# The decoder trunk's first loads merged with x transposed, and mem's norm factors summed on GpSimd

## The chip, the cores and the metric

One core of a Trainium2 chip runs the whole program; the metric is the device time of one execution in microseconds. Before the change three runs took 628.57, 625.1 and 627.83 us, median 627.83.

## The reference, cut to what matters

A decoder trunk of two layers on 256 tokens of width 1024. Each layer normalizes, mixes, adds, normalizes, and runs a gated feed-forward block:

```
xn = rms_norm(h, norm_mix[i]);  mn = rms_norm(mem, norm_mem[i])
mk, mv = split(mn @ w_mem_kv[i])                  # 4 memory heads, 256 memory tokens
proj = xn @ w_in                                  # q, k, v of 12 heads, memory queries, (layer 0) forget gates
self_out = fox_attention(...) or moba_attention(...)
h = h + concat(self_out, memory_attention(qm, mk, mv)) @ w_out[i]
gu = rms_norm(h, norm_ffn[i]) @ w_gate_up[i]
h = h + (silu(gate) * up) @ w_down[i]
```

where `rms_norm(x, g) = x * rsqrt(mean(x*x) + 1e-6) * g`. Layer 0 is the forgetting layer: its logits get a bias from the running sums of log-sigmoid gates. Everything is float32.

## The kernel before, in words

All weights come as one stream of units of about 1 MB, in the order of use; a unit fills one of four `raw` buffers. The tensor engine multiplies in a split form: each weight half-unit is copied by ScalarE to a rounded `hi` (L215) and VectorE forms `lo` = raw - hi (L216), and each product is three matmuls, hi by hi, lo by hi and hi by lo (`prod`, all at L178). Activations are split in the same way by `split_ps` (L237 on ScalarE, L238 on VectorE), scaled by the norm's gain. There are seven `hi` and seven `lo` buffers; `weights` splits five half-units ahead (AHEAD) and fetches three units ahead (FETCH). The norm's per-token factor is not applied to the operand: it is computed apart (`factor`: a ScalarE square with a sum at L243, VectorE L254, a GpSimd power at L256), turned into a row of factors for all partitions by `spread` (matmuls into `rsb_ps`, ScalarE L267), and multiplied into the products.

TensorE and SyncE (SP) run in the order in which the program is written. The order on ScalarE (ACT), VectorE (DVE) and GpSimd (POOL) is set ahead of time by a planner that puts what is ready first, and an engine never changes that order on the chip. SP issues the loads one after another, and a load whose buffer isn't free holds back all behind it.

Layer 0 runs on TensorE like this:
- eight warm matmuls on a zeroed tile (L737 clears it, after four clears of `mk` at L314);
- the value projection `v_ps`, 16 steps (eight row blocks k of x transposed, two token blocks t) of six matmuls. The stream's first unit is x transposed, loaded in four cuts; the value weights, units 1 to 4, are cut too, and cuts of the two are issued in turn. x's rows for the norm factors (`h`), the constants `sq` and the gate bias `bfg` come after unit 5;
- `qk_ps`, the first four heads' queries and keys (half-units of units 5 and 6), then `rsb_ps_x`;
- `mem_kv(0)`: memory keys and values `mk_ps`, `mv_ps`, from mem transposed (`x_mem`, unit 7, split at L237 and L238) and units 8 and 9. The gates' running sums (`F_ps`, `Fq_ps`) fall in the middle of it, at the second call of `step()`, which moves every generator in `active` on by one `yield`; the sums go to DRAM (`fd`, L490) and come back on all partitions (`fk`, three loads at L493);
- `qm_ps`, the memory queries; after its eight steps the last part of `mem_kv(0)`: mem's rows are loaded as a unit of their own (`U["mem"]`), squared on ScalarE (`junk_mem`, L243), and mem's factors give `rsb_ps_mem`; then `mk` is scaled (L349) and split in eight half-partition copies on ScalarE (L369, L370) and two differences (L372), the values are evacuated (L353), the memory queries are scaled (L535) and split (L362, and L364 on GpSimd and VectorE);
- the next `qk_ps` with the scores of the memory heads (`s_m`) and of the first self heads (`s_s`) between its steps, and so on; the bias of a head pair is four VectorE instructions at L510.

After some 133 us the feed-forward block of layer 0 begins, then layer 1; neither is touched by the change but for the buffers' size and what comes earlier or later from layer 0.

Of the kernel before, what the change touches and what calls it, by code (L numbers as in the profile page):

```python
# [45 lines left out]
HEAD = 384  # L46
WORK_BUFS = 7
PAIR_BUFS = 3
WARM = 8
FACTORS_AT = 6  # L50
# [28 lines left out]
class Plan:  # L79


    def __init__(self, a):
# [4 lines left out]
        U["xT"] = self.unit([xT], 0, KD, 0, S)  # L87
        for i in range(2):
# [3 lines left out]
            for u in range(4):  # L92
                U["vf", i].append(self.unit([w], 2 * u, 2, 2 * SW, nv))
            for g in range(3):
                if g == MEM_AT[i]:
                    if i == 0:
                        U["memT", 0] = self.unit([memT], 0, KD, 0, S)
                        self.mkv(a, 0)
                        self.blocks.append(a["mem"][0].reshape(NT, P, D).transpose(1, 0, 2).reshape(-1))
                        self.shapes.append((NT, 1, D))  # L100
                        U["mem"] = len(self.shapes) - 1
                    U["qm", i] = self.unit([w], 0, KD, 2 * SW + nv, MW)
# [36 lines left out]
def trunk(ctx: ExitStack, tc: tile.TileContext, plan, stream, x, gains, norm_final, b_fgate, square, out):  # L139
# [43 lines left out]
    raw_only = {U["xT"], U["memT", 0], U["memT", 1], U["mem"]}  # L183
# [3 lines left out]
    AHEAD, FETCH = 5, 3  # L187

    def fetch():
# [3 lines left out]
        raw = wp.tile([P, UNIT], F32, tag="raw", name=f"raw{i}", bufs=4)  # L193
# [12 lines left out]
    def split():  # L206
        i, k0, nk = halves[counts[1]]
        fetch_to(i + 1 + FETCH)
        sh = plan.shapes[i][1:]
        n = nk * sh[0] * sh[1]  # L210
        hi = wp.tile([P, HALF], F32R, tag="hi", name=f"hi{i}_{k0}", bufs=7)
        lo = wp.tile([P, HALF], F32R, tag="lo", name=f"lo{i}_{k0}", bufs=7)
        src = raws[i][:, k0:k0 + nk].rearrange("p a b c -> p (a b c)")
        for c0, c1 in ((0, HEAD), (HEAD, n)) if (i, k0) == (1, 0) else ((0, n),):
            nc.scalar.activation(hi[:, c0:c1], src[:, c0:c1], AF.Copy)  # L215
            nc.vector.tensor_sub(lo[:, c0:c1], src[:, c0:c1], hi[:, c0:c1].bitcast(F32))  # L216
# [75 lines left out]


# [22 lines left out]
    for mk in mks:  # L316
        no_lo(mk)
# [41 lines left out]
    def split_queries(dst, q):  # L359
# [3 lines left out]
        for a in range(2):  # L363
            ENG[a].tensor_sub(dst[HOME[1 - a], a], q[HOME[a]], dst[HOME[a], a].bitcast(F32))  # L364
# [68 lines left out]
    active = []  # L433

# [6 lines left out]
    def mixer(i, xs, rs):  # L441
# [11 lines left out]
        order = [(k, t) for k in range(KD) for t in range(NT)]  # L453
        if i == 1:
            order.sort(key=lambda kt: (kt[0] // 4, kt[1], kt[0]))
        for k, t in order:
            v_tile(k, t)
            if i == 0 and (k, t) == (FACTORS_AT, 1):
                rs.extend(factor(h[t_], f"x0{t_}") for t_ in range(NT))
        if i == 0:  # L460
            z = sp.tile([P, NT, H], F32, tag="z", name="z", bufs=1)
            for t in range(NT):
                nc.vector.scalar_tensor_tensor(z[:, t], vb[t][1].t[:, w0:w0 + H], rs[t], bfg, op0=ALU.mult, op1=ALU.add)
            na = sp.tile([P, NT, H], F32, tag="na", name="na", bufs=1)
            nc.vector.scalar_tensor_tensor(na, z, -1.0, z, op0=ALU.mult, op1=ALU.min)
            e = sp.tile([P, NT, H], F32, tag="e", name="e", bufs=1)
            nc.scalar.activation(e, na, AF.Exp)
            l = sp.tile([P, NT, H], F32, tag="l", name="l", bufs=1)
            nc.scalar.activation(l, e, AF.Ln, bias=1.0)
            lf = cp.tile([P, NT, H], F32, name="lf")  # L470
            nc.vector.scalar_tensor_tensor(lf, z, 0.0, l, op0=ALU.min, op1=ALU.subtract)
        for t in range(NT):
            for c in range(2):
                dst = vsb[t][:, 6 * c:6 * c + 6, 0:DH]
                src = vb[t][c].t[:, :w0].rearrange("p (a d) -> p a d", d=DH)
                if c == 0:
                    nc.scalar.activation(dst, src, AF.Copy, scale=rs[t])
                else:
                    nc.vector.tensor_scalar_mul(dst, src, rs[t])
# [3 lines left out]
        def gate_sums():  # L483
# [7 lines left out]
            for g in range(GATE_PARTS):  # L491
                hs = slice(g * (H // GATE_PARTS), (g + 1) * (H // GATE_PARTS))
                nc.sync.dma_start(fk[:, hs], fd[hs].unsqueeze(0).to_broadcast([P, H // GATE_PARTS, S]))  # L493
# [4 lines left out]
            nc.scalar.activation(fq.rearrange("p t h -> p (t h)"), gb.t[:, :NT * H], AF.Copy)  # L498

        def bias(h0):  # L500
# [7 lines left out]
            for a in range(2):  # L508
                for t, o in ((0, b0), (1, b)):
                    nc.vector.scalar_tensor_tensor(o[:, a], b[:, a, :(t + 1) * P], fq[:, t, h0 + a:h0 + a + 1], mask[:, P - t * P:],  # L510
                                                   op0=ALU.subtract, op1=ALU.add)
# [5 lines left out]
        def memory_heads():  # L517
# [269 lines left out]
```

## Time and profile before

| | us |
|---|---|
| median of three runs | 627.83 (625.1 to 628.57) |
| the profiled execution | 628.3 |
| its span, first to last instruction | 626.5 |
| busy in the span: PE, DVE, ACT, POOL | 609.5, 457.3, 392.6, 60.4 |
| mean granted TensorE clock | 0.992 |

The span is what the trace covers; 1.8 us of the profiled execution lie around it. A busy time is the time in which an engine has an instruction running, waiting for a port of the memory included.

### The profile page before, as it was taken

How to read it: one execution, taken by the hardware profiler on the slowest of the kernel's cores; microseconds unless marked ns; L12 is line 12 of the kernel's file. 1: busy time of each engine (PE TensorE's matmuls, PEld its weight loads, DVE VectorE, ACT ScalarE, POOL GpSimd, SP SyncE). 2: the span in 40 equal slices, each digit the busy share in tenths (PEclk: the TensorE clock that was granted, in tenths of full speed). 3: DMA queues.
4: the chain of work that ended last, by engine and by line, in shares of the span. 5: the costliest groups of instructions: out<-in, count | busy, mean ns of one | idle time of the engine just before them, and what ended most of it. 6: DMA issues, size and time to landing. Idle time of an engine off the chain costs nothing.

```text
span 626.5 us, 9569 instructions
## 1 busy us (share of the span) xinstructions
PE 609.5 (97%) x3636; PEld 536.2 (86%) x3636; DVE 457.3 (73%) x827; ACT 392.6 (63%) x734; POOL 60.4 (10%) x90
## 2 busy tenths in 40 slices
PE   7999899999999999999999999999999999999995
PEld 5999887778888888888899999877888888888884
DVE  5588899978676666668675589986876666676664
ACT  6679887666555555557466589875755555555542
POOL 2021345300000000000011033100000000000000
PEclk8999899999999999999999999999999999999999
DMA  8974812445555555555555633332455545555301
GB/s 293 390 283 166 347 69 85 146 173 202 199 174 179 194 196 202 194 177 176 210 186 194 215 140 126 135 134 68 169 201 202 186 176 181 198 201 202 136 0 67
DMA packets 17638, 112.31 MB, mean 179 GB/s; under 512 B 2220, under 2 KB 2744, under 8 KB 5432
## 3 DMA queue, kind: packets, MB, share of 16 engines
q1 hardware_dynamic: 17304, 111.42, 49.1%
q8 instruction: 28, 0.46, 0.3%
q10 hardware_dynamic: 288, 0.29, 0.1%
q14 instruction: 18, 0.15, 0.1%
HBM read 110.64 MB, written 1.06 MB: 178 GB/s over the span
## 4 chain that ended last, share of the span: by engine, by line
PE 83%; DVE 7%; ACT 6%; issue 2%; DMA 2%; POOL 0%; SPq 0%; POOLq 0%; ACTq 0%; DVEq 0%
PE gu L178 39%; PE d_acc L178 18%; PE qk_ps L178 8%; PE v_ps L178 6%; PE o_acc L178 4%; DVE lo L216 2%; DMA raw<-in_stream 2%; ACT hi L215 2%; PE s_s L178 1%; ACT p_s L406 1%; PE mv_ps L178 1%; PE qm_ps L178 1%; PE mk_ps L178 1%; PE s_m L178 1%; ACT xq L362 1%
## 5 line engine op out<-in xcount | busy, mean ns | idle before, releaser
L216 DVE TENSOR_TENSOR lo<-raw,hi 128x1024 fp32r<-128x1024 f32 (+3 forms) x201 | 240.6, 1204 | 70.6 <-ACT hi L215 65.6
L215 ACT ACTIVATE hi<-raw 128x1024 fp32r<-128x1024 f32 (+3 forms) x201 | 206.2, 1034 | 74.2 <-PE d_acc L178 47.0
L178 PE MATMUL gu<-x_ffn,hi 128*128 128x512 f32 x704 | 177.5, 392 | 0.0
L178 PEld LDWEIGHTS gu<-x_ffn,hi 128*128 128x128 f32 x704 | 126.3, 189 | 22.2
L178 PE MATMUL d_acc<-hi,h 128*128 128x512 f32 x348 | 107.1, 389 | 0.0
L178 PEld LDWEIGHTS gu<-x_ffn,lo 128*128 128x128 f32 x704 | 96.7, 190 | 8.1 <-ACT x_ffn L237 1.0
L178 PE MATMUL gu<-x_ffn,lo 128*128 128x256 f32 x704 | 100.5, 284 | 0.2
L178 PEld LDWEIGHTS d_acc<-hi,h 128*128 128x128 f32 x348 | 65.3, 188 | 13.6
L178 PE MATMUL qk_ps<-x_x,hi 128*128 128x256 f32 x384 | 73.7, 288 | 0.0
L178 PE MATMUL d_acc<-lo,h 128*128 128x512 f32 x174 | 67.7, 389 | 0.0
L178 PEld LDWEIGHTS qk_ps<-x_x,hi 128*128 128x128 f32 x384 | 62.1, 195 | 0.8 <-issue 0.8
L178 PE MATMUL qk_ps<-x_x,lo 128*128 128x256 f32 x192 | 55.0, 286 | 0.0
L642 ACT ACTIVATE gate<-gu 128x256 f32<-128x256 f32 x44 | 16.9, 384 | 57.6 <-PE gu L178 57.6
L178 PE MATMUL o_acc<-hi,x_hT 128*128 128x512 f32 x128 | 41.7, 404 | 0.6 <-DVE x_hT L235 0.3
L642 ACT ACTIVATE up<-gu 128x256 f32<-128x256 f32 x44 | 16.9, 385 | 40.0 <-PE gu L178 39.7
L178 PEld LDWEIGHTS d_acc<-lo,h 128*128 128x128 f32 x174 | 32.7, 188 | 6.8
L178 PEld LDWEIGHTS qk_ps<-x_x,lo 128*128 128x128 f32 x192 | 37.6, 196 | 0.0
L643 DVE TENSOR_TENSOR gate<-gu,gate 128x256 f32<-128x256 f32 x44 | 18.7, 424 | 25.8 <-ACT gate L642 25.8
L643 DVE TENSOR_TENSOR up<-gu,up 128x256 f32<-128x256 f32 x44 | 18.7, 425 | 25.1 <-ACT up L642 25.1
L178 PE MATMUL v_ps<-hi,x_x 128*128 128x384 f32 (+1 forms) x128 | 34.3, 350 | 1.7 <-ACT hi L215 1.7
L406 ACT ACTIVATE p_s<-p_s,nmax_s 128x128 f32<-128x128 f32 (+1 forms) x48 | 21.4, 446 | 11.8 <-DVE nmax_s L396 11.6
L178 PEld LDWEIGHTS o_acc<-hi,x_hT 128*128 128x128 f32 x128 | 22.8, 188 | 6.4 <-issue 1.3
(152 smaller groups left out, 752.3 us busy)
## 6 DMA issues: line engine op xcount, KB each, us to landing
raw<-in_stream SPq DMA_DIRECT2D x95, 1024.0 KB, 4.8
raw<-in_stream SPq DMA_DIRECT2D x4, 768.0 KB, 4.5
raw<-in_stream SPq DMA_DIRECT2D x2, 780.0 KB, 8.3
fk<-fd SPq DMA_DIRECT2D x3, 512.0 KB, 4.9
raw<-in_stream SPq DMA_DIRECT2D x3, 390.0 KB, 6.2
h<-in_x SPq DMA_DIRECT2D x2, 512.0 KB, 7.1
raw<-in_stream SPq DMA_DIRECT2D x1, 512.0 KB, 7.1
gfin<-in_norm_final SPq DMA_DIRECT2D x1, 512.0 KB, 3.7
```

The source lines that it names most:

```text
L178: nc.tensor.matmul(o, lhsT, rhs, start=self.fresh, stop=stop, skip_group_check=True)
L215: nc.scalar.activation(hi[:, c0:c1], src[:, c0:c1], AF.Copy)
L216: nc.vector.tensor_sub(lo[:, c0:c1], src[:, c0:c1], hi[:, c0:c1].bitcast(F32))
L362: nc.scalar.activation(dst[HOME[a], a], q[HOME[a]], AF.Copy)
L406: nc.scalar.activation(pr[:, a, c], src, AF.Exp, bias=nmax[:, a, j], scale=scale, accum_out=total[:, a, j])
L642: nc.scalar.activation(v[:, 1], b[s].t[:, S:], AF.Copy)
L643: nc.vector.tensor_add(v[:, 0], b[s].t[:, :S], v[:, 1])
```

## The change

- x transposed is no unit of its own any more: each of the four value units carries, for each row of weights, the 256 columns of x transposed ahead of the 780 of the weights (2,072 columns a unit, and `raw` grows from 2,048 to that). Unit 0 is loaded in two halves, the others whole. `split_first` splits x's row block between a half-unit's `hi` and its `lo`. SP issues the four units first, then `h`, `sq` and `bfg`.
- ACT and DVE follow the written order in layer 0's value stage: splitting runs at most two half-units ahead into the next stage, the values are evacuated before the gate's exponential and logarithm, and the factors of x are asked for at k = 2 and not 6. Warm matmuls: 12 for 8; GpSimd clears their tile before `mk`.
- The unit `mem` goes. Mem's squares come from mem transposed: on GpSimd eight products and seven sums of 128x256 (`mem_squares`), then two small matmuls by a column of minus ones add over the partitions (`mem_factors`). That is asked for after k = 1 of `qm_ps`, and the rest of `mem_kv(0)` after k = 4, where both came after k = 7.
- The three `fk` loads are issued two `step()` calls later, and the L510 instructions are queued behind the last split of the memory queries.

```
-WARM = 8
-FACTORS_AT = 6
+RAW = 2 * (S + SW + H)
+WARM = 12
+FACTORS_AT = 2
...
-        U["xT"] = self.unit([xT], 0, KD, 0, S)
...
+                cols = w[:, 2 * SW:2 * SW + nv]
+                if i == 0:
+                    cols = np.concatenate([xT, cols], axis=1)
+                U["vf", i].append(self.unit([cols], 2 * u, 2, 0, cols.shape[1]))
...
-                        U["mem"] = len(self.shapes) - 1
...
-        cuts = {0: [0, n // 8, n // 4, n // 2, n], 1: [0, HEAD, n // 2, n], 2: [0, n // 2, n]}.get(i, [0, n])
+        cuts = [0, n // 2, n] if i == 0 else [0, n]
...
             nc.scalar.activation(hi[:, c0:c1], src[:, c0:c1], AF.Copy)
+            if with_x and c0 == 0:
+                split_first(i, k0)
             nc.vector.tensor_sub(lo[:, c0:c1], src[:, c0:c1], hi[:, c0:c1].bitcast(F32))
...
-        while counts[1] < min(len(halves), ready[i, kk][2] + 1 + AHEAD):
+        while counts[1] < min(len(halves), ready[i, kk][2] + 1 + ahead[0]):
...
+    x0 = xposed("x0")
+    def split_first(i, kk):
+        k = 2 * U["vf", 0].index(i) + kk
+        split_ps(x0[0][:, k, :], x0[1][:, k, :], raws[i][:, kk, 0, :S], gT[:, k, 0:1])
...
+    def mem_squares():
+        w = cp.tile([P, 2, S], F32, name="squares")
+        for k in range(KD):
+            src = raws[U["memT", 0]][:, k, 0, :]
+            nc.gpsimd.tensor_mul(w[:, min(k, 1)], src, src)
+            if k > 0:
+                nc.gpsimd.tensor_add(w[:, 0], w[:, 0], w[:, 1])
+        return w[:, 0]
+    def mem_factors(sums):
+        b = bank("ms_mem")
+        for t in range(NT):
+            b.mm(b.t[:, 2 * t:2 * t + 2], sums[:, t * P:(t + 1) * P], prefix[:, P:P + 2], stop=True)
+        for t in range(NT):
+            me = sp.tile([P, 1], F32, tag="me", name=f"me_mem{t}")
+            nc.vector.tensor_scalar(me, b.t[:, 2 * t:2 * t + 1], -1.0 / D, EPS, op0=ALU.mult, op1=ALU.add)
+            rs = sp.tile([P, 1], F32, tag="rs", name=f"rs_mem{t}", bufs=8)
+            nc.gpsimd.tensor_tensor(rs, me, minus_half, op=ALU.pow)
+            rs_mem.append(rs)
...
         split_x(U["memT", i], 2 + i, xs, range(MEM_AHEAD))
+        if i == 0:
+            sums = mem_squares()
         yield
...
-            fetch_to(U["mem"] + 1)
-            rs_mem.extend(factor(raws[U["mem"]][:, t, 0], f"mem{t}") for t in range(NT))
+            mem_factors(sums)
+            yield
...
+        with tc.manual_schedule(engines={ACT, DVE}) if i == 0 else nullcontext():
...
+                if i == 0:
+                    ahead[0] = min(AHEAD, KD + 1 - k)
...
-            for g in range(GATE_PARTS):
-                hs = slice(g * (H // GATE_PARTS), (g + 1) * (H // GATE_PARTS))
-                nc.sync.dma_start(fk[:, hs], ...)
             gb = bank("Fq_ps")
...
+            yield
+            yield
+            for g in range(GATE_PARTS):
+                hs = slice(g * (H // GATE_PARTS), (g + 1) * (H // GATE_PARTS))
+                nc.sync.dma_start(fk[:, hs], ...)
...
+                    with tc.issue_after(mem_done[i]):
+                        nc.vector.scalar_tensor_tensor(o[:, a], b[:, a, :(t + 1) * P], fq[:, t, h0 + a:h0 + a + 1],
+                                                       mask[:, P - t * P:], op0=ALU.subtract, op1=ALU.add)
...
+                if i == 0 and k in (1, 4):
+                    next(g, None)
                 if k == 3:
                     step()
-            if i == 0:
-                next(g, None)
...
-    (x0, x1, x2, x3), (w0, w1, w2), (w3, w4) = list(fetch()), list(fetch()), list(fetch())
-    for f in (w0, x0, w1, x1, w2, w3, x2, w4, x3):
-        f()
-    fetch_to(6)
+    fetch_to(4)
     load_x()
     with tc.manual_schedule(engines={PE, SP}):
         warm = ap.tile([P, 512], BF16, tag="work", name="warm", bufs=WORK_BUFS)
         nc.gpsimd.memset(warm, 0.0)
+        for mk in mks:
+            no_lo(mk)
```

## Rows read from the trace of the kernel before

**Rows 1.** The page, part 1: busy time, share of the span and instructions of each engine.
```profile
PE 609.5 (97%) x3636; PEld 536.2 (86%) x3636; DVE 457.3 (73%) x827; ACT 392.6 (63%) x734; POOL 60.4 (10%) x90
```

**Rows 2.** Busy time in stretches of layer 0's first part. Columns: the stretch and its length in us, busy us and instructions of PE, PE's weight loads, DVE, ACT and POOL, the granted TensorE clock, the DMA engines' busy share and GB/s.
```profile
8.36:26.90 18.54, 18.54 (x94) 18.23 (x95) 12.30 (x20) 13.25 (x21) 1.11 (x2) 0.91 0.98 386
26.90:38.40 11.50, 11.50 (x98) 11.50 (x96) 9.19 (x17) 9.00 (x16) 0.00 (x0) 1.00 0.79 301
38.40:52.00 13.60, 13.60 (x113) 13.01 (x112) 9.40 (x13) 11.24 (x22) 4.04 (x5) 1.00 0.57 219
52.00:64.08 12.08, 12.08 (x102) 11.88 (x100) 10.31 (x11) 10.70 (x19) 3.02 (x4) 1.00 0.68 239
64.08:66.06 1.98, 0.00 (x1) 0.00 (x1) 1.49 (x4) 1.86 (x6) 0.85 (x2) 1.00 1.01 397
66.06:81.00 14.94, 14.94 (x113) 14.93 (x114) 13.94 (x51) 11.70 (x32) 4.26 (x8) 0.89 0.68 283
81.00:113.00 32.00, 29.99 (x210) 24.62 (x208) 30.83 (x83) 26.30 (x65) 15.61 (x16) 1.00 0.28 100
```

**Rows 3.** The same view, cut at the places where DVE's load changes.
```profile
29.00:39.70 10.70, 10.70 (x92) 10.70 (x91) 7.98 (x13) 8.43 (x17) 0.00 (x0) 1.00 0.77 295
39.70:55.60 15.90, 15.90 (x132) 15.31 (x131) 11.69 (x16) 14.19 (x27) 4.98 (x6) 1.00 0.58 216
55.60:81.00 25.40, 23.42 (x185) 23.21 (x184) 23.29 (x62) 20.65 (x49) 7.19 (x11) 0.93 0.69 272
```

**Rows 4.** The timeline of the first 15 us, all engines: start in us, length in us, engine, line, operation, what is written and read, shape, number of instructions, and in brackets the idle time ahead of it with what ended it.
```profile
0.89 1.35 POOL L314 MEMSET mk<- 64x256 f32 x4
...
2.76 3.33 PE L178 MATMUL warm_ps<-warm 128*128 128x512 bf16 x8 [2.76 <-POOL warm L737]
...
3.40 0.52 ACT L215 ACTIVATE hi<-raw 128x384 fp32r<-128x384 f32 x1 [0.94 <-DMA raw<-in_stream]
...
3.98 0.51 ACT L237 ACTIVATE x_x<-raw,gT 128x256 fp32r<-128x256 f32 x1
...
7.38 0.51 ACT L237 ACTIVATE x_x<-raw,gT 128x256 fp32r<-128x256 f32 x1 [2.90 <-DMA raw<-in_stream]
...
8.36 0.63 PE L178 MATMUL v_ps<-hi,x_x 128*128 128x396 f32 x2 [1.75 <-ACT hi L215]
...
12.93 0.51 PE L178 MATMUL v_ps<-hi,x_x 128*128 128x384 f32 x2
...
14.00 0.51 PE L178 MATMUL v_ps<-hi,x_x 128*128 128x384 f32 x2
```

**Rows 5.** The view of rows 2 for one microsecond after that stall.
```profile
10.00:11.00 1.00, 1.00 (x5) 1.00 (x5) 1.00 (x2) 0.99 (x4) 0.00 (x0) 0.50 1.03 423
```

**Rows 6.** DMA issues of three short windows, with KB and us from issue to landing: the stream's first load (issued at 0.73), its eighth (4.60), and mem transposed (16.89).
```profile
raw<-in_stream SPq DMA_DIRECT2D x1, 192.0 KB, 2.6
...
raw<-in_stream SPq DMA_DIRECT2D x1, 390.0 KB, 6.4
...
raw<-in_stream SPq DMA_DIRECT2D x1, 1024.0 KB, 13.9
```

**Rows 7.** The chain of work that ended last, in order of time: start, us, what.
```profile
8.36 18.68 PE v_ps L178 x93
27.05 11.51 PE qk_ps L178 x96
...
54.26 5.95 DMA raw<-in_stream
```

**Rows 8.** Timelines of ACT (the first two rows) and of DVE from 28 to 40 us, columns as in rows 4.
```profile
29.70 1.99 ACT L215 ACTIVATE hi<-raw 128x1024 fp32r<-128x1024 f32 x2
31.59 3.30 ACT L237 ACTIVATE x_mem<-raw,gT 128x256 fp32r<-128x256 f32 x8
...
30.77 2.36 DVE L216 TENSOR_TENSOR lo<-raw,hi 128x1024 fp32r<-128x1024 f32 x2 [0.76 <-ACT hi L215]
33.05 3.25 DVE L238 SCALAR_TENSOR_TENSOR x_mem<-raw,gT,x_mem 128x256 fp32r<-128x256 f32 x8
36.22 2.35 DVE L216 TENSOR_TENSOR lo<-raw,hi 128x1024 fp32r<-128x1024 f32 x2
```

**Rows 9.** Timelines of POOL (the first three rows) and of DVE, where both work on operands in the on-chip memory; the last row is one in which POOL had nothing to do.
```profile
42.03 1.60 POOL L364 TENSOR_TENSOR xq<-qk,xq 64x256 fp32r<-64x256 f32 x1 [18.32 <-ACT xq L362]
43.71 0.80 POOL L372 TENSOR_TENSOR xk<-qk,xk 64x256 fp32r<-64x256 f32 x1
46.05 0.73 POOL L364 TENSOR_TENSOR xq<-qk,xq 64x256 fp32r<-64x256 f32 x1 [1.53 <-ACT xq L362]
...
41.82 1.22 DVE L216 TENSOR_TENSOR lo<-raw,hi 128x1024 fp32r<-128x1024 f32 x1
43.07 0.84 DVE L364 TENSOR_TENSOR xq<-qk,xq 64x256 fp32r<-64x256 f32 x1
...
109.94 0.42 DVE L372 TENSOR_TENSOR xk<-qk,xk 64x256 fp32r<-64x256 f32 x1
```

**Rows 10.** ACT's timeline, one row, then two rows of the waits (who waited for whom: us in total, times, longest us) of PE up to 170 us and of SP up to 70 us.
```profile
50.16 1.05 ACT L243 ACTIVATE junk_mem<-raw 128x1024 bf16<-128x1024 f32 x1
...
PE s_m L178 <- POOL xqm L364: 2.0, 1, 2.0
...
SPq L198 <- DVE me_mem L254: 8.2, 1, 8.2
```

More of the change, by code (lines that the diff above doesn't have):

```diff
@@ L12 @@
-from contextlib import ExitStack
+from contextlib import ExitStack, nullcontext
 import numpy as np
@@ L182, in trunk @@
     U = plan.U
-    raw_only = {U["xT"], U["memT", 0], U["memT", 1], U["mem"]}
+    raw_only = {U["memT", 0], U["memT", 1]}
     halves = [(i, j * (sh[0] // 2), sh[0] // 2) for i, sh in enumerate(plan.shapes) if i not in raw_only for j in range(2)]
@@ L187, in trunk @@
     AHEAD, FETCH = 5, 3
+    ahead = [AHEAD]
     def fetch():
@@ L451, in v_tile @@
                 prod(vb[t][c], vb[t][c].t[:, :cols[c][1]], tok(xs, k, t), (wh[:, 0, cs], wl[:, 0, cs]), k == KD - 1)
[L453 to L459, printed above, removed]
-        if i == 0:
-            z = sp.tile([P, NT, H], F32, tag="z", name="z", bufs=1)
-            for t in range(NT):
[L463 to L479, printed above, removed]
+        with tc.manual_schedule(engines={ACT, DVE}) if i == 0 else nullcontext():
+            order = [(k, t) for k in range(KD) for t in range(NT)]
+            if i == 1:
+                order.sort(key=lambda kt: (kt[0] // 4, kt[1], kt[0]))
+            for k, t in order:
+                if i == 0:
+                    ahead[0] = min(AHEAD, KD + 1 - k)
+                v_tile(k, t)
+                if i == 0 and (k, t) == (FACTORS_AT, 1):
+                    rs.extend(factor(h[t_], f"x0{t_}") for t_ in range(NT))
+            if i == 0:
+                z = sp.tile([P, NT, H], F32, tag="z", name="z", bufs=1)
+                for t in range(NT):
+                    nc.vector.scalar_tensor_tensor(z[:, t], vb[t][1].t[:, w0:w0 + H], rs[t], bfg, op0=ALU.mult, op1=ALU.add)
+            for t in range(NT):
+                for c in range(2):
+                    dst = vsb[t][:, 6 * c:6 * c + 6, 0:DH]
+                    src = vb[t][c].t[:, :w0].rearrange("p (a d) -> p a d", d=DH)
+                    if c == 0:
+                        nc.scalar.activation(dst, src, AF.Copy, scale=rs[t])
+                    else:
+                        nc.vector.tensor_scalar_mul(dst, src, rs[t])
+            if i == 0:
+                na = sp.tile([P, NT, H], F32, tag="na", name="na", bufs=1)
+                nc.vector.scalar_tensor_tensor(na, z, -1.0, z, op0=ALU.mult, op1=ALU.min)
+                e = sp.tile([P, NT, H], F32, tag="e", name="e", bufs=1)
+                nc.scalar.activation(e, na, AF.Exp)
+                l = sp.tile([P, NT, H], F32, tag="l", name="l", bufs=1)
+                nc.scalar.activation(l, e, AF.Ln, bias=1.0)
+                lf = cp.tile([P, NT, H], F32, name="lf")
+                nc.vector.scalar_tensor_tensor(lf, z, 0.0, l, op0=ALU.min, op1=ALU.subtract)
@@ L480, in mixer @@
+        ahead[0] = AHEAD
         if i == 0:
@@ L685, in finish @@
         c = NFC - 1
-        oo = wp.tile([P, UNIT], F32, tag="raw", name="o", bufs=4)
+        oo = wp.tile([P, RAW], F32, tag="raw", name="o", bufs=4)
         o = [oo[:, t * D:(t + 1) * D] for t in range(NT)]
@@ L728, in finish @@
         nc.scalar.dma_start(out[0, P:S, first], o[1][:, first])
-    (x0, x1, x2, x3), (w0, w1, w2), (w3, w4) = list(fetch()), list(fetch()), list(fetch())
-    for f in (w0, x0, w1, x1, w2, w3, x2, w4, x3):
-        f()
-    fetch_to(6)
+    woken = sp.tile([P, 1], F32, tag="woken", name="woken", bufs=1)
+    nc.scalar.activation(woken, minus_half, AF.Copy)
+    fetch_to(4)
     load_x()
@@ L746, in trunk @@
             if i == 1:
-                gfin = wp.tile([P, UNIT], F32, tag="raw", name="gfin", bufs=4)[:, :D]
+                gfin = wp.tile([P, RAW], F32, tag="raw", name="gfin", bufs=4)[:, :D]
                 nc.sync.dma_start(gfin, norm_final.rearrange("(o d) -> o d", o=1).to_broadcast([P, D]))
```

28 lines of the change are left out of this document (12 added, 16 removed).

## The prediction

> **What bounds it now.** I read the busy shares first: PE is busy for 97% of the span, DVE for 73%, ACT for 63%, POOL for 10% [rows 1], so whatever the change gives must come from PE's idle or slow time, or from an engine that makes PE wait. The table by stretch shows that layer 0's first 113 us are not one regime. Up to 64 us PE is busy without a break while the granted clock is full, except at the start [rows 2]. Then PE stands still from 64.08 to 66.06, and the next stretch has a mean clock of 0.89. From 81 to 113 DVE is busy 30.83 of 32.00 us and PE 29.99: there the two bound together. The timeline shows the start: the warm matmuls run from 2.76, the first value matmuls find their data, and then PE idles 1.75 us before 8.36, because ACT waited 2.90 us for a piece of x [rows 4]. After that idle the clock stands at half (1.2 GHz) [rows 5]. The waits name the second hole: memory scores wait 2.0 us for GpSimd's part of the memory queries' split, and SP had waited 8.2 us for the buffer of mem's rows [rows 10]. In the chain the value stage holds 18.68 us and a load that lands at 60.21 stands in the middle of the second hole's history [rows 7].
>
> **The sum** is made against the profiled execution, 628.3 us, 0.5 above the median of the runs. About 0.5% (3.1 us) is what a measurement of this kernel can tell from no change.
>
> **The front: -2.9 us for PE.** Warm: POOL's clears of `mk` (1.35) move behind the warm tile's, so the warm matmuls start at 2.76 - 1.35 = 1.4; eight took 3.33, twelve take 5.0 and end at 6.4 [rows 4]. Data: the first load of 192 KB landed 2.6 us after its issue at 0.73, thus at 3.3 [rows 6]; the first half unit has 518 KB, 326 KB more, which at 386 GB/s [rows 2] take 0.9, thus 4.2. ACT's two instructions (0.52, 0.51) make the first operands ready at 5.2, before the warm matmuls end. So PE starts at 6.4. A step is 1.07 (12.93 to 14.00, [rows 4]), sixteen are 17.1: 23.5. Later row blocks come at 518 KB in 1.4 us against 2.14 of PE work, so they keep ahead; I add 0.5 for slow first pieces and take 24.0, against 26.9 before. No idle, so the half clock after it should go too; that is inside this difference. Bounds: without the 0.5, -3.4. If loads start as slowly as they did, unit 1 (2.1 MB into the stream) lands where the eighth load did, 4.60 + 6.4 = 11.0 [rows 6]; split 1.4 later, six blocks of 2.14 and 1 us of late `lo` end at 26.2: -0.7.
>
> SP issues five large loads with no wait, so fewer issues cost nothing; `h`, `sq`, `bfg` go behind 4.2 MB, landing at about 18 by the same rate, and the factors asked for at k = 2 stand on ACT ahead of two half-units that PE needs at 24: hidden. The two evacuations that now stand ahead of the gate's exponential put the next `hi` 0.6 later relative to PE: it started at 29.70, 2.8 after the value stage [rows 8], and starts at 24.0 + 2.8 + 0.6 = 27.4. So ACT and DVE gain only 2.3 here.
>
> **Mem's squares: 15 GpSimd instructions against DVE.** No row has a 128x256 product on GpSimd; the nearest is a difference of 64x256 over the same 256 columns, 0.73 [rows 9]. GpSimd is idle, so 15 by 0.73 = 11 us are hidden for GpSimd itself. But look at rows 9: a POOL instruction issued at 42.03 took 1.60, not 0.73; DVE's `lo` ran until 43.04, so POOL ran about 0.60 after it. DVE's next 64x256 difference took 0.84, not 0.42, and so did the one after it. Whoever comes second waits, and they alternate. The Trainium skill, SBUF — State Buffer, Who interferes with whom, says that GpSimd and a VectorE instruction with two SBUF inputs share one port pair as an exclusive lock, held for the whole instruction; the trace agrees in kind. By that rule taken whole, a hold of 0.73 would make the term below 10.2 and the end 1.8 later.
>
> The squares begin when mem transposed lands: at 16.89 + 13.9 = 30.8 before [rows 6], about 29 with the earlier start. At that time DVE is in its longest run of two-input work: two `lo`, eight `x_mem`, two `lo` [rows 8]. Next to POOL an `x_mem` costs 0.60 + 0.28 = 0.88 for 0.41, a `lo` 1.69 for 1.18. I count 14 of 15 as holds: 14 x 0.60 = 8.4 us of DVE. Ends: 0 if they fall in its idle time, 10.9 at 15 full lengths of 0.73. PE's price depends on the planned order. PE wants the first memory weights' `lo` at 24.0 + 11.5 [rows 7] + 0.6 = 36.1; DVE has the second `lo` at 31.3; with three `x_mem` ahead it is ready at 35.6, with five at 37.4, with all eight (as before) at 40.0. I take five, +1.3, since the weights' landing falls in the middle of the eight; bounds 0 and 3.9, the latter with 1.6 for a half clock after it, as after the hole at 64.
>
> **Mem's factors earlier: up to -3.6 for PE.** ACT loses two squares of 1.05 and their reads [rows 10], 2.3 in all; the 1 MB load and SP's wait of 8.2 go. `mk`'s copies are released after k = 4, three of eight steps of a 5.7 us stage, 2.1 us sooner. The memory queries' split was 2.0 late; 2.3 + 2.1 cover that, so the hole goes, and with it the half clock that follows it (0.11 of 14.94 us, 1.6 lost [rows 2]). The two small matmuls are at most four of 0.18, a sixth of a step. But PE now waits in order, between k = 1 and k = 4, for two powers of GpSimd, at most 0.73 each by the nearest row, behind two small DVE instructions: 2.1 us of PE work against about 2, so 0 to 1 of a new wait, if a `lo` stands ahead of them on DVE. Bounds of the part: 0 and -3.6. The `fk` loads two steps later and L510 behind the queries' split: each takes bias work out of the way of those queries; `fk` is not needed before the scores at 71, so nothing.
>
> **What DVE lets through.** PE alone: -2.9 + 1.3 - 3.6 = -5.2. But DVE must also reach 113 sooner, as nothing but 1.2 of 32 us is idle in that stretch. DVE: starts 2.3 sooner, carries 8.4 more, and can take that up in its idle time from 29 to 81: 2.7 + 4.2 + 2.1 = 9.0 [rows 3], most of it waits for ACT, which is 2.3 lighter and no longer blocked by a landing. I take 8 of 9: -2.3 + 8.4 - 8.0 = **-1.9**. DVE is the later of the two, so it sets the sum: 628.3 - 1.9 - 0.5 = **625.9**. With 6 of the idle taken up it is 627.9, with all 9.0 it is 624.9, and with 12 holds in place of 14 besides, 623.7.
>
> **Rivals.**
> 1. **GpSimd costs DVE nothing.** If the squares run mostly beside instructions with one operand there, or in DVE's idle time, the 8.4 goes and so does PE's 1.3: PE moves by -6.5, DVE by -2.3 and some 4 of the idle, -6.3; less about 0.8 that the stretch from 81, where both are bound, takes back, -5.5: **622.3**. For it: those 9.0 us of idle. Against it: both start on the same landing.
> 2. **The lock passes through (slower).** Place: DVE from 29 to 45. Price: 8.4 and the PE hole at the first memory product. If the idle takes up only 2.5, because the waits for ACT only move: -2.3 + 8.4 - 2.5 = +3.6, **631.4**. It decides when less than 3.0 us of the 9.0 is absorbed. For it: the order of rows 8, all eight `x_mem` ahead of the memory weights. The Trainium skill, SBUF — State Buffer, Who interferes with whom, speaks for it with its lock for the whole instruction.
> 3. **The front does not get earlier:** -0.7 instead of -2.9, as a load of 390 KB took 6.4 us to land [rows 6]: 625.9 + 2.1 = **628.0**.
>
> **Numbers.** Forecast 0.45, first rival 0.30, second 0.15, third 0.10. Faster by over 0.5% (below 624.7): nearly all of rival 1 (0.29) and a little over a quarter of the forecast (0.12), 0.41. Slower (above 631.0): two thirds of rival 2 (0.10) and 0.05 of the forecast, where the hole of 3.9 and its half clock come on top. Same: 0.44. The range goes from 621.0, a little under rival 1, to 631.0, which leaves out most of rival 2.
>
> **What would show it.** Right: the value stage ends near 24.0 with no PE idle before it and a full clock from 9 to 12; POOL's squares take 0.9 to 1.7 each beside DVE; `x_mem` on DVE 0.8 to 0.9; a hole in PE of about a microsecond at the first `mk_ps`; none before `s_m`; PE waits on DVE between 75 and 108 longer than before. Wrong: squares of 0.73 and `x_mem` of 0.48, or a first landing after 6.4, or a hole before `s_m` that stays.

## The result, and the profile after

The change made the kernel slower: 630.37 us (629.75 to 630.78) against 625.87 of the kernel before in the same comparison, a ratio of 1.0061 [1.0045, 1.0077] (the ratio, with its 95% interval, is taken over the single runs, so it is not exactly that of the medians). The forecast was 625.9. The profiled execution of the changed kernel took 630.15 us, its span is 628.3. PE is busy longer than before, DVE and POOL too [rows 1]:

```profile
PE 611.4 (97%) x3644; PEld 536.0 (85%) x3644; DVE 461.9 (74%) x827; ACT 390.7 (62%) x731; POOL 74.1 (12%) x105
```

**By stretch** (columns as in [rows 2]; the cuts are those of before, moved by the 3 us that the front gained, up to the memory scores. From the third row on the stages end later than their cuts: the memory keys and values at 52.9, the memory queries at 60.9, and the first memory scores come at 66.6):

```profile
5.40:23.60 18.20, 17.91 (x97) 17.07 (x97) 12.24 (x21) 13.47 (x23) 1.08 (x2) 1.00 0.93 386
23.60:35.20 11.60, 11.60 (x98) 11.60 (x97) 10.31 (x16) 10.97 (x18) 7.52 (x10) 1.00 0.81 326
35.20:48.90 13.70, 11.35 (x79) 10.56 (x78) 13.04 (x13) 6.54 (x16) 10.60 (x10) 0.88 0.54 211
48.90:61.30 12.40, 11.63 (x95) 11.24 (x95) 9.08 (x12) 8.18 (x12) 1.06 (x2) 1.00 0.78 294
61.30:66.00 4.70, 4.70 (x41) 4.70 (x40) 1.78 (x4) 4.14 (x10) 1.76 (x3) 1.00 1.04 411
66.00:81.00 15.00, 13.16 (x109) 12.72 (x108) 14.56 (x47) 12.74 (x33) 4.67 (x8) 1.00 0.27 104
```

The value stage now ends near 23.6 at full clock, where it ended at 26.90 with a mean clock of 0.91. The hole before the memory scores is gone. But the third stretch, which had no idle before, lost 2.35 us of PE and has a clock of 0.88, and the stretch from 66 lost 1.84.

**The front**, from the timeline of the first microseconds (columns as in [rows 4]):

```profile
1.34 4.17 PE L178 MATMUL warm_ps<-warm 128*128 128x512 bf16 x12 [1.34 <-POOL warm L782]
...
4.41 0.52 ACT L219 ACTIVATE hi<-raw 128x384 fp32r<-128x384 f32 x1 [1.74 <-DMA raw<-in_stream]
...
5.38 0.97 PE L178 MATMUL v_ps<-hi,x_x 128*128 128x384 f32 x2
```

Warm matmuls end at 5.51 and the first value matmul is in at 5.38: the idle of 1.75 us is gone.

**The waits** of PE from 3 to 135 us (us in total, times, longest), where [rows 10] had one of 2.0 for the memory queries:

```profile
PE mk_ps L178 <- DVE lo L222: 2.4, 1, 2.4
PE qk_ps L178 <- ACT p_m L441: 1.8, 2, 0.9
PE s_s L178 <- DVE pT_s L456: 1.4, 1, 1.4
PE rsb_ps_mem L178 <- POOL rs_mem L352: 0.7, 1, 0.7
```

**Where the squares run**, DVE's timeline first (it answers to [rows 8]; all eight `x_mem` still stand ahead of the memory weights' four `lo`), then POOL's:

```profile
28.40 1.77 DVE L222 TENSOR_TENSOR lo<-raw,hi 128x1024 fp32r<-128x1024 f32 x1
30.09 6.62 DVE L244 SCALAR_TENSOR_TENSOR x_mem<-raw,gT,x_mem 128x256 fp32r<-128x256 f32 x8
36.63 6.52 DVE L222 TENSOR_TENSOR lo<-raw,hi 128x1024 fp32r<-128x1024 f32 x4
43.08 1.27 DVE L606 TENSOR_TENSOR qk<-qk_ps,rsb_x 128x512 f32<-128x512 f32 x2
...
50.15 6.90 DVE L222 TENSOR_TENSOR lo<-raw,hi 128x1024 fp32r<-128x1024 f32 x6 [0.66 <-ACT hi L219]
56.97 0.21 DVE L350 TENSOR_SCALAR me_mem<-ms_mem 128x1 f32<-128x1 f32 x2
```

```profile
27.05 1.19 POOL L338 TENSOR_TENSOR squares<-raw 128x256 f32<-128x256 f32 x2 [8.32 <-DMA raw<-in_stream]
...
34.89 0.68 POOL L338 TENSOR_TENSOR squares<-raw 128x256 f32<-128x256 f32 x1
35.64 0.78 POOL L340 TENSOR_TENSOR squares<-squares 128x256 f32<-128x256 f32 x1
...
40.48 1.59 POOL L340 TENSOR_TENSOR squares<-squares 128x256 f32<-128x256 f32 x1
```

An `x_mem` takes 0.83 us where it took 0.41, a `lo` 1.63 where it took 1.18.

### The profile page after: what moved, and what is told of

It reads as the page before. It is cut to its first block, busy times and chain, and to the rows that moved or that the text cites. A ratio compares the mean times of both kernels' runs of the same rounds, so it can differ in the third digit from the quotient of the medians.

```text
span 628.3 us, 9587 instructions
## 1 busy us (share of the span) xinstructions
PE 611.4 (97%) x3644; PEld 536.0 (85%) x3644; DVE 461.9 (74%) x827; ACT 390.7 (62%) x731; POOL 74.1 (12%) x105
## 4 chain that ended last, share of the span: by engine, by line
PE 76%; DVE 13%; ACT 5%; issue 3%; DMA 1%; POOL 0%; SPq 0%; POOLq 0%; DVEq 0%; ACTq 0%
PE gu L178 39%; PE d_acc L178 18%; DVE lo L222 5%; PE o_acc L178 5%; PE v_ps L178 4%; PE qk_ps L178 4%; ACT hi L219 1%; DMA raw<-in_stream 1%; PE mv_ps L178 1%; DVE p_s L431 1%; PE mk_ps L178 1%; ACT xq L396 1%; PE o_s L178 1%; DVE x_mem L244 1%; DVE p_m L445 1%
## 5 line engine op out<-in xcount | busy, mean ns | idle before, releaser
L178 PE MATMUL qk_ps<-x_x,hi 128*128 128x256 f32 x384 | 72.4, 284 | 1.8 <-ACT p_m L441 1.8
L178 PEld LDWEIGHTS qk_ps<-x_x,hi 128*128 128x128 f32 x384 | 60.9, 191 | 3.0 <-ACT p_m L441 2.3
L327 POOL MEMSET xk<- 64x256 f32 x24 | 7.4, 308 | 200.0 <-PE d_acc L178 178.9
L262 POOL TENSOR_TENSOR rs_f<-me_f,minus_half 128x1 f32<-128x1 f32 x5 | 2.7, 553 | 223.5 <-DVE me_f L260 223.5
```

The source lines that it names most:

```text
L178: nc.tensor.matmul(o, lhsT, rhs, start=self.fresh, stop=stop, skip_group_check=True)
L262: nc.gpsimd.tensor_tensor(rs, me, minus_half, op=ALU.pow)
L327: nc.gpsimd.memset(dst[HOME[1 - a], a, S:].bitcast(F32), 0.0)
```

## The experiments

Theory A: the loss is the port that GpSimd and VectorE share. GpSimd's reads make VectorE's instructions longer, VectorE falls behind, and TensorE waits for it. Rivals: the front's new order costs it; GpSimd's own lateness does (the buffer of mem transposed freed late); or the planner's other moves do. The median of the kernel before was 626.1 to 626.7 us in the comparisons below, each with 11 to 23 runs of it.

### Each half of the change alone

`e1_rows_of_mem` takes the mem part back (mem's rows as a unit again, squared on ScalarE after the memory queries) and keeps the front:

```
-            sums = mem_squares()
...
-            mem_factors(sums)
+            fetch_to(U["mem"] + 1)
+            rs_mem.extend(factor(raws[U["mem"]][:, t, 0], f"mem{t}") for t in range(NT))
```

> The changed kernel with its mem part undone: mem's rows are a unit again, squared on ScalarE, and the end of the memory stage comes after the eighth step of the memory queries; the merged loads, the written order in the value stage and the later gate loads stay. Held (the squares on GpSimd hold VectorE up, and the front's 3.2 us are real): the hole before the first memory product (2.35 us in the changed kernel) and the half clock after it go, x_mem on VectorE falls from 0.88 to 0.41 us each, and the time is 622 to 624, about 3 below the 625.9 of before. Rival A (the written order, L555 behind the memory queries and the later gate loads make it slower): stays at 629 to 631. Rival B (an earlier value stage only waits later): 625 to 627.

Measured: 625.61 us, ratio 0.9983 [0.997, 0.9995]. The hole at the first memory key is gone, but the time misses the 622 to 624 of "Held" and lies in the band of rival B: the earlier value stage mostly waits later. Against an undisturbed execution of before (`e5_before_again`, below) the first memory scores start 1.6 us earlier, at 62.6 for 64.2, and the feed-forward block 0.4 later, at 130.2 for 129.8.

`e2_squares_only` is the kernel before with the mem part alone:

```
+            sums = mem_squares()
...
-            rs_mem.extend(factor(raws[U["mem"]][:, t, 0], f"mem{t}") for t in range(NT))
+            mem_factors(sums)
+            yield
...
+                if i == 0 and k in (1, 4):
+                    next(g, None)
```

> The kernel before with the mem part of the change alone: squares of mem transposed on GpSimd, factors asked for after steps 1 and 4 of the memory queries, no unit of mem's rows. Held: VectorE's x_mem at 0.88 and its lo at 1.63 while GpSimd squares, a hole of 2 to 4 us before the second memory product near 39 us and a half clock behind it; the hole before s_m goes; 628 to 631. Rival A: 624 to 626, since this part only takes work off ScalarE and the load queue. Rival B says nothing of it.

Measured: 630.29 us, ratio 1.0059 [1.0037, 1.0081]. So the mem part is the whole loss. Eight `x_mem` took 6.60 us there, and PE waited 2.7 us for `lo` at the first memory key.

### GpSimd busy, but reading nothing

`e3_clears_for_squares` puts clears in place of the squares (mem's factors are constants then); `e12_more_clears` has 24 of them, so that GpSimd stays busy and holds the buffer as long as in the changed kernel:

```
-        for k in range(KD):
...
-            nc.gpsimd.tensor_mul(w[:, min(k, 1)], src, src)
...
+        nc.gpsimd.tensor_mul(w[:, 0, 0:1], src[:, 0, 0, 0:1], src[:, 0, 0, 0:1])
+        for k in range(15):
+            nc.gpsimd.memset(w.rearrange("p a s -> p (a s)"), 1.0)
+        nc.gpsimd.tensor_mul(w[:, 0, 0:1], src[:, 7, 0, 0:1], src[:, 7, 0, 0:1])
```

> The changed kernel with the fifteen products and sums on GpSimd replaced by fifteen clears of 128x512 that write and read nothing (one column of mem transposed is still read ahead of them and behind them, so that they run at the same time); mem's factors are then constants. GpSimd is busy as long, at about 0.5 us each. Held, in the form that the reads are what holds VectorE: x_mem at 0.41, no hole at the first memory product, 622 to 625. If any GpSimd work there holds VectorE (the port as such): x_mem at 0.7 to 0.9 and 629 to 631. Rival A: 629 to 631.

For `e12_more_clears`, against that run:

```
-        for k in range(15):
+        for k in range(24):
```

> The run with clears in place of the squares, with 24 clears instead of 15, so that GpSimd is busy and holds mem transposed's buffer until about 42 us, as long as in the changed kernel, and still reads nothing but one column at either end (mem's factors stay constants). Theory A (the loss is the lock: VectorE's instructions get longer, and that lag reaches TensorE): x_mem stays at 0.41, no hole at the first memory key, 624.4 to 625.5 us, within 1 us of the run with 15 clears. Theory B (the loss comes through GpSimd's own lateness: the buffer that it frees late, for which SP waits, and the queries' and keys' differences behind it): 627.5 to 630 us, with waits of TensorE for late weights or for the first heads between 45 and 66 us.

Measured: 624.56 us, ratio 0.9966 [0.9954, 0.9978], and with 24 clears 624.69, ratio 0.9965 [0.9953, 0.9977]. DVE's timeline with 15 clears, then POOL's:

```profile
28.60 1.22 DVE L222 TENSOR_TENSOR lo<-raw,hi 128x1024 fp32r<-128x1024 f32 x1
29.74 3.25 DVE L244 SCALAR_TENSOR_TENSOR x_mem<-raw,gT,x_mem 128x256 fp32r<-128x256 f32 x8
32.90 4.62 DVE L222 TENSOR_TENSOR lo<-raw,hi 128x1024 fp32r<-128x1024 f32 x4
37.45 1.28 DVE L606 TENSOR_TENSOR qk<-qk_ps,rsb_x 128x512 f32<-128x512 f32 x2
...
44.51 6.90 DVE L222 TENSOR_TENSOR lo<-raw,hi 128x1024 fp32r<-128x1024 f32 x6 [0.66 <-ACT hi L219]
51.33 0.21 DVE L350 TENSOR_SCALAR me_mem<-ms_mem 128x1 f32<-128x1 f32 x2
```

```profile
27.52 8.72 POOL L339 MEMSET squares<- 128x512 f32 x15
```

GpSimd is busy at the same time, and `x_mem` takes 0.41 again. In the run with 24, SP waited longer for POOL than in the changed kernel (the waits of SP from 20 to 70 us, that run, then the changed kernel to 70 us):

```profile
SPq L199 <- POOL squares L340: 6.3, 1, 6.3
```

```profile
SPq L199 <- POOL squares L338: 3.7, 1, 3.7
```

and it cost nothing. So the late buffer falls as a rival. GpSimd being busy is not the cause either; what the squares have and the clears lack is that they read their operands.

### Half the squares

`e6_half_squares` squares blocks 0 to 3 only:

```
-        for k in range(KD):
+        for k in range(KD // 2):
...
-            nc.vector.tensor_scalar(me, ..., -1.0 / D, EPS, ...)
+            nc.vector.tensor_scalar(me, ..., -2.0 / D, EPS, ...)
```

> The changed kernel with half of GpSimd's squaring: blocks 0 to 3 of mem transposed only (7 operations instead of 15; mem's factors come from half its columns). Theory A (the port's lock, paid once per GpSimd operation): 7 holds of 0.6 us instead of 14, about four of the x_mem remainders at 0.83 us and the rest at 0.41, the four lo near 1.2 us, TensorE's hole ahead of the first memory key under 0.5 us and no half clock after it: 624 to 626.5 us, 4 to 6 us below the changed kernel, that is most of the loss, since a hole opens only once the cover is used up. Theory B (each hold costs the span its share): half of the loss of 5.8 us against the clears, that is 627 to 628 us.

Measured: 626.75 us, ratio 1.001 [1.0002, 1.0019], between the two bands. DVE (its second row answers to the second row of the changed kernel's timeline):

```profile
28.54 1.77 DVE L222 TENSOR_TENSOR lo<-raw,hi 128x1024 fp32r<-128x1024 f32 x1
30.23 4.95 DVE L244 SCALAR_TENSOR_TENSOR x_mem<-raw,gT,x_mem 128x256 fp32r<-128x256 f32 x8
35.10 4.62 DVE L222 TENSOR_TENSOR lo<-raw,hi 128x1024 fp32r<-128x1024 f32 x4
```

Against the clears DVE carries 1.70 + 0.55 = 2.25 us more and the time is 2.2 us longer; with all fifteen it is 3.37 + 1.90 + 0.55 = 5.8 us more and 5.8 us longer. What was expected of A, that a hole opens only once a cover is used up, fell: the charge reaches the end one to one at both doses, though the hole at the first memory key is only 0.3 here (0.8 more is waited at mem's factors).

### Another order on VectorE, another place for the squares

`e9_lo_between` gives VectorE the order that the prediction had assumed; `e11_tail_later` then asks for the last part of `mem_kv(0)` after k = 6 instead of 4:

```
...
+                last[0] = split_x(U["memT", 0], 2, xm[0], range(3))
+            with tc.issue_after(last[0]) if (i, k0) in ((first[0], 0), (first[0], 2), (first[1], 0)) else nullcontext():
+                last[0] = nc.vector.tensor_sub(lo[:, c0:c1], src[:, c0:c1], hi[:, c0:c1].bitcast(F32)).ins
+            if i == first[0]:
+                with tc.issue_after(last[0]):
+                    last[0] = split_x(U["memT", 0], 2, xm[0], (3, 4) if k0 == 0 else (5, 6, 7))
```

> The changed kernel, squares on GpSimd as they are, but VectorE's order around them is the one that the prediction had assumed: three x_mem remainders, the memory weights' first lo, two x_mem, the second lo, the last three x_mem, then the other two lo (the changed kernel had all eight x_mem ahead of the first lo). Theory A (the loss is TensorE's hole at the first memory key and the half clock after it, and the rest of VectorE's charge is taken up by its idle time, as predicted): no hole at about 36 us, full clock, 625.5 to 627 us, some 4 us below the changed kernel. Theory B (VectorE's charge from the port reaches the end in any order, as a row of smaller holes): 628.5 to 630.5 us, with new waits of TensorE for VectorE between 38 and 66 us that sum to 2 us or more.

For `e11_tail_later`, against that run:

```
-                if i == 0 and k in (1, 4):
+                if i == 0 and k in (1, 6):
```

> The run with the lo between the x_mem, and the last part of mem_kv(0) asked for after k = 6 of the memory queries instead of k = 4, so that TensorE has two more steps (2.9 us) to do while it waits for mem's factors (it waited 4.34 us there, with 3.4 us of half clock after it). The holds on VectorE stay. Theory A (the loss is in the place where the wait falls, and the lag of VectorE is taken up if nothing asks for it early): a hole of at most 1.5 us, full clock, and no new one before the memory scores: 625 to 626.5 us. Theory B (VectorE's lag only moves: the wait comes back one place later, before the memory scores, where the scaled keys and the queries' split are late): 627.5 to 629 us, with a hole of 2 us or more between 60 and 68 us.

Measured: 628.94 us, ratio 1.0046 [1.0029, 1.0063], and 628.2, ratio 1.0036 [1.0023, 1.0049]. The hole at the first memory key is gone in both, and the wait came back at mem's factors. First PE's wait in the one, then DVE's rows behind it, then PE's wait in the other:

```profile
PE rsb_ps_mem L178 <- POOL rs_mem L362: 4.3, 1, 4.3
```

```profile
52.48 3.50 DVE L227 TENSOR_TENSOR lo<-raw,hi 128x1024 fp32r<-128x1024 f32 x3 [0.67 <-ACT hi L219]
55.90 0.22 DVE L360 TENSOR_SCALAR me_mem<-ms_mem 128x1 f32<-128x1 f32 x2
```

```profile
PE rsb_ps_mem L178 <- POOL rs_mem L362: 2.6, 1, 2.6
```

Both times lie where theory B put them: the lag only moves. The place was not B's: a single hole at the factors, not a row of small ones, and in the second run the same place again, not the memory scores. `me_mem` stands behind three `lo` in an order that is fixed ahead of time; that this order is part of the cause is read from the timeline, and no run changed it.

The two runs end 1.4 and 2.2 us before the changed kernel, but not because VectorE took the charge up. The table has what the squares added to the eight `x_mem` and the six `lo` around them, and when PE starts the first memory scores and layer 0's feed-forward block (us; the charge against the run with 15 clears):

| run | charge | first `s_m` | feed-forward | span |
|---|---|---|---|---|
| 15 clears | 0 | 61.3 | 129.3 | 622.8 |
| half the squares | 2.2 | 63.2 | 131.4 | 625.0 |
| changed kernel | 5.8 | 66.6 | 134.8 | 628.3 |
| `e9_lo_between` | 5.8 | 67.6 | 133.6 | 627.1 |
| `e11_tail_later` | 5.4 | 66.2 | 132.6 | 626.1 |

At the memory scores the last four are 1.9, 5.3, 6.3 and 4.9 us later than the clears, so nearly the whole charge has passed by then (in `e9_lo_between` more than it, as half clock followed its hole: the mean clock from 48.9 to 61.3 us is 0.86). What the last two win over the changed kernel, they win behind that place, where PE waits 0.9 us in them for `p_m` and 0.8 for `pT_s`, and 1.8 and 1.4 in the changed kernel.

`e10_squares_later` holds the squares back behind the four `lo`:

```
+    def mem_squares(behind):
+        with tc.issue_after(behind):
+            nc.vector.memset(w[:, :, 0:1], 0.0)
...
+                if i == 0 and k == 0:
+                    sums = mem_squares(lo_of[ready[U["mkv", 0][1], 2][2]])
```

> The changed kernel, with GpSimd's fifteen operations held back until VectorE has done the eight x_mem and the four lo of the memory weights (a 2-column clear on VectorE, behind the last of these lo, writes where the squares go first). Same holds, other neighbours: lo, then differences of 64x256. Theory A (only the place of the holds was bad): x_mem 0.41 again, no hole at the first memory key, 625 to 627 us, if the sums are there in time for the two small matmuls at about 50 us. Theory B (the charge reaches the end wherever it falls while TensorE is busy): 628 us or more, with holes in TensorE from 40 to 56 us; the longer hold of mem transposed's buffer would show as a late load of a later unit.

Measured: 637.4 us, ratio 1.0178 [1.0159, 1.0198], the slowest of all. `x_mem` took 3.25 for eight and the first memory key did not wait, as A had it, but the sums were late:

```profile
PE ms_mem L178 <- POOL squares L343: 7.5, 1, 7.5
PE rsb_ps_mem L178 <- POOL rs_mem L355: 2.2, 1, 2.2
```

The time is above the 628 of B, but A's condition was not met, so this run does not decide. It shows the lock from the other side: beside five `lo` that ran without a break, squares took 1.48 to 1.75 us, and 0.60 to 0.72 after them.

### What is left without GpSimd's squares

`e4_rows_early` keeps the front and the earlier factors, but loads mem's rows as a unit and squares them on ScalarE at k = 5 of the memory keys; `e7_front_undone` is the kernel before with that arrangement of mem; `e8_no_gate_moves` is `e4_rows_early` without the two gate moves (the later `fk` loads, and L555, the L510 of before, behind the queries' split).

```
-            sums = mem_squares()
...
+                if i == 0 and k == 5:
+                    fetch_to(U["mem"] + 1)
+                    rs_mem.extend(factor(raws[U["mem"]][:, t, 0], f"mem{t}") for t in range(NT))
...
-            mem_factors(sums)
```

> The changed kernel with mem's rows as a unit again, squared on ScalarE in the middle of the memory keys (k = 5), and the rest of the memory stage after step 4 of the memory queries as in the change, without the wait for two powers of GpSimd. Held: no hole at the first memory product, none before rsb_ps_mem (0.74 in the changed kernel), none or a small one before s_m; 621 to 623.5, the best of the four. Rival A: 629 to 631. Rival B: 625 to 627.

For `e7_front_undone`, against the kernel before:

```
-            fetch_to(U["mem"] + 1)
-            rs_mem.extend(factor(raws[U["mem"]][:, t, 0], f"mem{t}") for t in range(NT))
+            yield
...
+                if i == 0 and k == 5:
+                    fetch_to(U["mem"] + 1)
+                    rs_mem.extend(factor(raws[U["mem"]][:, t, 0], f"mem{t}") for t in range(NT))
...
+                if i == 0 and k in (1, 4):
+                    next(g, None)
```

> The first loads, their order, the value evacuation and the gate as in the kernel before, with mem's rows squared on ScalarE early, as in the run that has rows early. Tells what the front is worth when mem's tail does not take it back. Theory A (the front's 3 us pass to the end when nothing later waits): 625 to 626.5 us, 2.5 to 3.5 us above the run with rows early. Theory B (the front is worth about 1 us whatever stands behind it): 623.5 to 624.5 us.

For `e8_no_gate_moves`, against `e4_rows_early`:

```
-            yield
-            yield
...
-                    with tc.issue_after(mem_done[i]):
+                    if True:
```

> The run with rows early, without the two small moves in the gate (the later loads of the gate's rows, and the biased scores held until memory's queries are split). Theory A (both moves cost and bring nothing): 622.4 to 623.4 us. Theory B (they keep transfers or VectorE work off a wait before the first scores): 1 to 3 us above, with a hole at the queries of memory or at the first scores.

Measured, in the same order: 622.9 us, ratio 0.9942 [0.9922, 0.9961], as expected and faster than both kernels; 624.62, ratio 0.9972 [0.996, 0.9984]; 623.02, ratio 0.9948 [0.9936, 0.996]. The front makes 1.7 us between the first two, which is between the two bands. Of that 1.1 are there at the first memory scores (61.1 for 62.1); the rest arises behind them, where PE waits 0.8 for `nmax_s` ahead of `pT_m` in `e7_front_undone` and not in `e4_rows_early`, and whether it belongs to the front is not shown. The gate moves are worth 0.1, inside theory A's band. The longest waits of PE in `e4_rows_early`, from 3 to 135 us:

```profile
PE qk_ps L181 <- ACT p_m L444: 0.9, 1, 0.9
PE s_s L181 <- DVE pT_s L459: 0.8, 1, 0.8
```

### The execution that the prediction was summed on

`e5_before_again` is another profile of the kernel before.

> The kernel before, unchanged: a second profile of it. Theory A (the profiled execution that the prediction was summed on stood above the median by chance, because TensorE's half clock lasted longer in it): this profile shows other lengths of the stretches at half clock, and a span up to 2 us below 626.5 us. Theory B (the execution was typical): the same stretches (about 9.1 to 12.5 and 67.1 to 70.5 us) and a span within 0.5 us of 626.5.

Measured: 624.95 us, span 623.1, and otherwise the same picture: the holes of 1.5 us at the start and 2.0 before the memory scores are there, but the clock behind them is full. The profile of before first, then this one (columns as in [rows 2]):

```profile
9.10:12.50 3.40, 3.40 (x11) 3.40 (x12) 3.25 (x5) 2.88 (x6) 0.00 (x0) 0.50 1.03 425
67.10:70.50 3.40, 3.40 (x19) 3.40 (x18) 3.34 (x9) 3.37 (x9) 0.00 (x0) 0.50 1.02 426
```

```profile
9.10:12.50 3.40, 3.40 (x21) 3.40 (x20) 3.39 (x6) 2.99 (x6) 0.00 (x0) 1.00 1.06 428
64.20:67.60 3.40, 3.40 (x28) 3.40 (x29) 3.30 (x8) 3.35 (x6) 0.79 (x1) 1.00 1.02 408
```

Half the clock (1.2 GHz) in two stretches of 3.4 us is 1.7 us lost in each, and 3.4 is the difference of the two spans. Whether such a stretch follows a hole differs from one execution to the next. Of the 23 runs of before in that comparison, five with a mean granted clock of 0.996 to 0.998 took 624.7 to 625.1 us, two with 0.992 took 628.26 and 628.35, and sixteen with 0.994 or 0.995 lay between. Theory A of this run held in kind; its "up to 2 us" was 3.4.

## Why the prediction was wrong, by its steps

A gain of 2.4 us on its execution was forecast, and a loss of 4.5 between the medians was measured. The 630.4 lies inside the range, near its upper end, but the kernel got slower where a gain was forecast. The signs that were named for being right came nearly all (the value stage near 24 at full clock, `x_mem` at 0.83, no hole before the memory scores), and the second rival shares them; none was named for the uptake, the term that decided between the two. (One small sum is off: the third rival's 2.1 is 2.2 by its own numbers, which decides nothing.)

**The base.** The prediction put its execution 0.5 above the median. It was 1.8 above the median of the later runs, since it had two stretches at half clock. Two terms counted their removal as a gain in full, though an execution of before has them only sometimes.

**The front, -2.9.** Against the execution that was summed it was right: the first `qk_ps` stood at 26.88 and stands at 23.72, and the clock is full. Part of that is luck: PE started at 5.38 and not at 6.4, and the stage took 18.3 us and not 17.6. Against the execution without half clock (24.99, from the timeline of `e5_before_again`) it is -1.3; the two runs with mem's rows early put it at 1.1 at the memory scores and 1.7 at the end.

**The squares.** The mechanism was as predicted. GpSimd's 0.68 to 0.81 beside an `x_mem` answers to the 0.73; `x_mem` 0.83 to the forecast 0.88, `lo` 1.63 to 1.69. The charge was 5.8 us, not 8.4, and the size of a hold was wrong, not their number: the first two products ran while VectorE was idle, and the other thirteen each held one of the eight `x_mem` and five `lo`, close to the 14 counted. A hold cost 0.45 on average, not 0.60. The prediction's own prices (0.88 for 0.41, 1.69 for 1.18) are 0.47 and 0.51 and give 6.3 for these thirteen; its sum took 0.60 instead. The Trainium skill, SBUF — State Buffer, Who interferes with whom, says that a VectorE instruction with two SBUF inputs does not contend with a GpSimd instruction that only writes; the clears agree (x_mem 3.25 for eight beside 8.72 us of clears). Its lock for the whole instruction is more than the trace shows: strict turns would make each `x_mem` 0.41 + 0.73 = 1.14, and it took 0.83.

**The step that failed: "can take that up in its idle time from 29 to 81 ... I take 8 of 9."** Nothing was taken up. From the clears to the changed kernel the group of six `lo` moved from 44.51 to 50.15 and `me_mem` from 51.33 to 56.97: 5.64 us in both, the whole charge. From 29 to 81 us VectorE is idle for 7.34 us in the changed kernel, and for 7.36 with clears. Two reasons stand in the timelines. DVE's idle lay elsewhere than its charge: in the run with clears it works almost without a break from 28.6 to 51.5, and its longer idle comes only behind `me_mem` (2.63). And the little idle between, 0.66 ahead of the six `lo`, is a wait for ACT's `hi`, which moved along because ACT was itself waiting for DVE. ACT's timelines, changed kernel and then clears:

```profile
43.79 0.86 ACT L396 ACTIVATE xq<-qk 64x256 fp32r<-64x256 f32 x2 [6.30 <-DVE qk L606]
```

```profile
38.16 0.86 ACT L396 ACTIVATE xq<-qk 64x256 fp32r<-64x256 f32 x2 [0.59 <-DVE qk L606]
```

The other copies of queries and keys and then the `hi` stand behind that row in ACT's order. This is the second rival, "the waits for ACT only move", to the letter; it had 0.15. That its price of 631.4 comes so near is partly luck: its charge was too high by 2.6, and 2.5 of it were to be taken up and were not.

**The hole at the first memory key, +1.3.** It was 2.35 us, and half clock behind it, 1.7 more (columns as in [rows 2]):

```profile
38.40:41.70 3.30, 3.30 (x16) 3.30 (x17) 3.30 (x3) 0.00 (x0) 3.14 (x3) 0.50 0.19 25
```

The slack was to be read from the first consumer's date. With clears the first of the four `lo` is ready near 34.1, and PE takes it up at 35.9, so 1.8 us were there. In the changed kernel it is ready at 38.3. The prediction took five `x_mem` ahead of it, where [rows 8] had eight and the planner knew nothing of the holds. That order alone would not have saved the time: in the run with the `lo` between, this hole is gone and the memory scores come no earlier.

**Mem's factors, up to -3.6.** The hole before the memory scores went, 2.0 us, and the new wait was 0.74, inside the 0 to 1 that was given. Part of the gain was given back behind it. PE waits 1.8 us in two pieces for ACT's `p_m`, also with clears (1.6) and once (0.9) in the fastest kernel. No term had that. ACT is late there, but that this comes of the hole's going is not shown: `e1_rows_of_mem` has a hole of 1.6 before the memory scores and waits 0.9 for `p_m` too, and `e8_no_gate_moves` has no such wait. In the second of the two pieces, two of the second head pair's `p_m` stand behind a `hi` of 1.05 us (ACT, changed kernel):

```profile
77.51 0.46 ACT L441 ACTIVATE p_m<-s_m,nmax_m 128x256 f32<-128x256 f32 x1
...
77.95 1.05 ACT L219 ACTIVATE hi<-raw 128x1024 fp32r<-128x1024 f32 x1
78.92 0.47 ACT L441 ACTIVATE p_m<-s_m,nmax_m 128x256 f32<-128x256 f32 x1
```

**The sum.** Span of before without half clock 623.1; front -1.3; hole and half clock at the first memory key +4.1; the hole before the scores -2.0; the factors +1.6 (the wait 0.7, the matmuls of `mem_factors` 0.3, and 0.5 by which `rsb_ps_mem` took longer); `p_m` +1.8; and +0.8 from there to the feed-forward block, 0.6 of it PE's wait for `pT_s` (1.4 for 0.8): 628.1, and 628.3 was measured. The holes are pieces of one lag and not separate costs: in `e9_lo_between` the hole at the first memory key is gone, and the one at the factors is 4.3 for 0.7. The first rival, no cost on DVE, had 622.3 and is what the clears made real: 624.6. Its gains were counted from the disturbed base (1.8), and the waits for `p_m` (1.6) were not counted; that these two make the difference is argued, not tested.

What stays open: why the waits for `p_m` differ from kernel to kernel (the planner's order changes with every edit), and what decides whether a hole brings half clock.

## What to carry to other kernels

Count slack from the place of a charge to the first consumer that is due behind it, and not as the sum of an engine's idle time over a long stretch: idle that is a wait for another engine moves along when that engine waits for the first. An order that is fixed ahead of time does not answer to contention: DVE's order is the same with squares and with clears. So a charge of some us on a tight engine passed almost whole here, in the three arrangements that were tried. And compare kernels at a place behind the edit as well as at the end, as a later stretch can change too. Last, profile the base more than once: here two executions of one kernel differed by 3.4 us, not far from the 4.5 that the change cost, and the granted clock says so in one row.

## What the hardware showed that was not expected

GpSimd clears that read nothing cost VectorE nothing, 15 of 0.58 us beside eight `x_mem` of 0.41, where products and sums of half the size doubled them. A hole of about 2 us brought half clock in one execution of the kernel before and not in another; the hole of 2.35 brought it in the profile of the changed kernel, whose ten runs all had a mean granted clock of 0.993 to 0.996.
